# Attention scores of a two-branch decoder trunk: two 128-row products a head in place of three 64-row ones

## The chip, the cores and the metric

One Trainium2 chip, of which one core runs the kernel. The time is the device time of one execution in microseconds; the kernel before took 1076.8 us (median of three runs, 1076.33 to 1079.78).

## What is computed

One layer of a trunk: a half-weighted SwiGLU feed-forward, a token mixer, a second feed-forward, on 512 tokens of width 1024 with 16 meta tokens ahead. Only the mixer bears on the change. It projects the normalised tokens to queries, keys and values of eight "fox" heads (forgetting attention over all earlier tokens) and to eight query and two key/value heads of a sliding window of 128, all of width 64:

```
qa = rms_norm(qa.reshape(b, p, FOX_HEADS, HEAD_DIM), fox_q_norm)
ka = rms_norm(ka.reshape(b, p, FOX_HEADS, HEAD_DIM), fox_k_norm)
...
s = jnp.einsum('bqhd,bkhd->bhqk', qi, k, preferred_element_type=jnp.float32) * scale
s = s + cqi[..., :, None] - c_k[:, :, None, :]
...
s_band = jnp.einsum('bnqgrd,bnkgd->bngrqk', qb, kb, preferred_element_type=jnp.float32) * scale + bias_band[None]
...
y = jax.nn.sigmoid(ga) * (o_fox @ w_branch_fox) + jax.nn.sigmoid(gb) * (o_swa @ w_branch_swa)
```

## The kernel before

Everything is float32, and TensorE is fed with a shorter type. So each operand a is kept as two: its part aH (`hi`, line 130: ScalarE rounds it) and its rest aL = a - aH (`lo`, line 136: VectorE subtracts). A product a b is the sum of three in one PSUM bank: aH bH + aH bL + aL bH (`prod`, line 297).

The mixer's work is a list of small steps. A chunk (`tok_chunk`, line 1025) projects 256 columns for the five token tiles, two steps (half tiles) of twelve 128-row products each; the values (`v_chunk`), the keys and queries (`qk_chunk`, line 1120) and the sliding keys and values (`kv_chunk`) are chunks. The last step of a query or key chunk (`finish`) transposes the normalised heads on TensorE, so that a head's 64 features lie in rows: two heads share 128 rows, the even one in rows 0 to 63, the odd one in 64 to 127. From there the parts are rounded and the rests taken, 128 rows at a time, with the gains.

A fox unit (`fox_pair`, line 1249) takes a pair p of heads and two query blocks: the wide ones (ip = 1) see blocks 2 and 3, the narrow ones 0 and 1. There are four wide and four narrow units, p = 0 and 1 on the first chunks (f0), p = 2 and 3 on the second (f1). A sliding unit (`swa_unit`, line 1431) takes four heads and one block; there are eight. A unit's `scores` are products of 64 rows; VectorE then adds the biases and finds the minimum of the negated scores (L1310, L1460), ScalarE takes the exponent (L1209), VectorE divides (L1212), TensorE transposes the result (L1350, L1473), it is split in part and rest, and the values are multiplied (L1359 to L1365, L1488, L1490). Fox scores are written in lines 1289 to 1299 with the two heads in turn; the sliding ones go through `prod`, so they stand under L301, L302 and L304 with kH, kL and qH in their names.

`weave` (line 57) mixes the units' steps with steps of chunks that are needed later (`fills`, line 1628): TensorE has projections to do while a unit's softmax runs on the other engines. There are four such parts: the first two pairs of heads, the other two, and two groups of four sliding heads. A scheduler then sets each engine's order, and each engine goes through its own in that order. SyncE's queue loads the weights (L206, L252); a load waits there until its buffer is free, and what is behind it waits too.

Two buffers matter besides: zA (8 rows of 512 a partition, tag z), where the gates are put from the third part on and whose last two rows held masks, and oA (tag o), the attention's result.

## Time and profile before

| | us |
|---|---|
| runs | 1076.33, 1076.8, 1079.78 |
| the profiled execution | 1077.47 |
| its span, first to last instruction | 1075.7 |
| TensorE busy | 1064.0 |
| VectorE busy | 891.9 |
| ScalarE busy | 655.0 |
| granted TensorE clock (share of full speed) | 0.997 |

Times in the trace count from the span's start. PE is TensorE, PEld its weight loads, DVE VectorE, ACT ScalarE, POOL GpSimd, SP SyncE. In the order of time a row is start, length, engine, line, operation, output and input tiles, forms; a matmul's length includes its way through the array, so neighbours overlap, and the step from start to start tells what one costs. "64*128" is a product of 64 rows. In the windows stand the window, its length, and busy time with the number of instructions for PE, PEld, DVE, ACT and POOL, then the granted clock, the DMA share and GB/s. A row of waits has who waited, at what line, for whom: us in total, times, longest. A row of a group has its count, busy time, mean ns of one, and idle time before it. A DMA row has its count, size, and median time to landing.

### The profile page before, as it was taken

What the parts mean: (1) busy time and instruction counts of PE and PEld (TensorE: products, weight loads), DVE (VectorE), ACT (ScalarE), POOL (GpSimd) and SP (SyncE); (2) the same over time, 40 slices, a digit from 0 to 9 for tenths busy, and PEclk for the clock granted to TensorE, in tenths of its full rate; (3) what the DMA queues carried; (4) which work ended last, traced back from release to release, by engine and by line L of the source; (5) the groups of instructions that cost most, each with busy time, mean ns of one, the idle gap of its engine ahead of it and who ended that gap; (6) DMA issues with size and microseconds to landing.
All of it is one profiled execution on the core that took longest, in us unless ns stands there. A gap on an engine that the chain in (4) does not pass through costs nothing.

```text
span 1075.7 us, 22259 instructions
## 1 busy us (share of the span) xinstructions
PE 1064.0 (99%) x8515; PEld 1031.8 (96%) x8515; DVE 891.9 (83%) x1725; ACT 655.0 (61%) x1235; POOL 212.9 (20%) x281
## 2 busy tenths in 40 slices
PE   9999999999999999999999999999999999999998
PEld 8999999999999998999878799999999999999998
DVE  6988878988889678789897799878989788887895
ACT  7676456656666455556667866555665466745664
POOL 3011111121124442232200110001122211221120
PEclk9999999999999999999999999999999999999999
DMA  8787777688776414222311874557688777887763
GB/s 281 195 217 167 187 195 192 154 215 219 174 181 179 124 61 119 76 65 64 98 59 40 239 177 134 186 193 201 166 205 182 184 193 177 180 194 196 158 125 102
DMA packets 112570, 173.57 MB, mean 161 GB/s; under 512 B 10880, under 2 KB 59264, under 8 KB 112208
## 3 DMA queue, kind: packets, MB, share of 16 engines
q1 hardware_dynamic: 74032, 122.03, 35.5%
q0 software_dynamic: 29040, 37.83, 22.6%
q10 hardware_dynamic: 9392, 12.29, 3.7%
q8 instruction: 66, 1.08, 0.4%
q14 instruction: 40, 0.33, 0.1%
HBM read 167.89 MB, written 6.32 MB: 162 GB/s over the span
## 4 chain that ended last, share of the span: by engine, by line
PE 47%; DVE 4%; ACT 2%; DMA 1%; issue 1%; POOL 0%; ACTq 0%; DVEq 0%; POOLq 0%
PE ps L301 8%; PE ps L304 8%; PE ps L302 8%; PE pt L301 7%; PE pt L302 7%; PE pt L304 7%; DMA raw<-in_wout_dram 1%; DVE wl L140 1%; ACT wh L133 1%; ACT t L1209 1%; DVE pL L140 1%; PE ps L1473 0%; PE ps L1936 0%; DVE S L140 0%; PE pt L1473 0%
## 5 line engine op out<-in xcount | busy, mean ns | idle before, releaser
L301 PE MATMUL ps<-x,wh 128*128 128x256 f32 (+2 forms) x768 | 220.1, 287 | 0.1
L302 PE MATMUL ps<-x,wh 128*128 128x256 f32 (+2 forms) x768 | 219.4, 286 | 0.5 <-DVE x L142 0.4
L304 PE MATMUL ps<-x,wl 128*128 128x256 f32 (+2 forms) x768 | 219.4, 286 | 0.0
L140 DVE TENSOR_TENSOR wl<-raw,wh 128x1024 fp32r<-128x1024 f32 (+3 forms) x125 | 149.9, 1200 | 40.7 <-ACT wh L133 39.5
L133 ACT CAST wh<-raw 128x1024 fp32r<-128x1024 f32 (+3 forms) x125 | 128.4, 1029 | 86.1 <-PE ps L302 50.9
L301 PEld LDWEIGHTS ps<-x,wh 128*128 128x128 f32 x768 | 145.3, 189 | 1.4 <-ACT pt L529 0.3
L302 PEld LDWEIGHTS ps<-x,wh 128*128 128x128 f32 x768 | 145.1, 189 | 1.4 <-DVE x L142 0.9
L304 PEld LDWEIGHTS ps<-x,wl 128*128 128x128 f32 x768 | 145.2, 189 | 0.9
L301 PE MATMUL pt<-x,wh 128*128 128x256 f32 (+2 forms) x424 | 125.3, 297 | 0.2 <-ACT wh L133 0.2
L304 PE MATMUL pt<-x,wl 128*128 128x256 f32 (+2 forms) x424 | 124.5, 294 | 0.0
L302 PE MATMUL pt<-x,wh 128*128 128x256 f32 (+2 forms) x392 | 112.5, 287 | 0.0
L133 ACT CAST wh<-tc 128x1024 fp32r<-128x1024 f32 (+1 forms) x70 | 71.8, 1026 | 64.3 <-DVE tc L234 55.1
L140 DVE TENSOR_TENSOR wl<-tc,wh 128x1024 fp32r<-128x1024 f32 (+1 forms) x70 | 83.5, 1193 | 32.4 <-ACT wh L133 32.2
L301 PE MATMUL ps<-acts,wh 128*128 128x264 f32 (+1 forms) x352 | 100.5, 285 | 0.1
L304 PE MATMUL ps<-acts,wl 128*128 128x264 f32 (+1 forms) x352 | 99.8, 284 | 0.0
L302 PE MATMUL ps<-acts,wh 128*128 128x264 f32 (+1 forms) x352 | 99.5, 283 | 0.0
L140 DVE TENSOR_TENSOR wl<-rawC,wh 128x1024 fp32r<-128x1024 f32 (+1 forms) x70 | 84.2, 1202 | 5.9 <-ACT wh L133 5.5
L133 ACT CAST wh<-rawC 128x1024 fp32r<-128x1024 f32 (+1 forms) x70 | 71.6, 1023 | 22.8 <-PE pt L302 16.9
L301 PEld LDWEIGHTS pt<-x,wh 128*128 128x128 f32 x424 | 79.9, 189 | 2.6 <-ACT wh L133 0.4
L304 PEld LDWEIGHTS pt<-x,wl 128*128 128x128 f32 x424 | 79.8, 188 | 2.1
L302 PEld LDWEIGHTS pt<-x,wh 128*128 128x128 f32 x392 | 73.7, 188 | 0.6
L301 PEld LDWEIGHTS ps<-acts,wh 128*128 128x128 f32 x352 | 66.5, 189 | 0.7 <-DVE h2T L918 0.3
(442 smaller groups left out, 3241.8 us busy)
## 6 DMA issues: line engine op xcount, KB each, us to landing
rawC<-in_w1i_dram SPq DMA_DIRECT2D x20, 512.0 KB, 4.5
raw<-in_w1i_dram SPq DMA_DIRECT2D x40, 256.0 KB, 4.0
raw<-in_w2i_dram SPq DMA_DIRECT2D x40, 256.0 KB, 3.5
rawC<-in_w2i_dram SPq DMA_DIRECT2D x20, 512.0 KB, 4.4
raw<-in_wm_dram SPq DMA_DIRECT2D x18, 512.0 KB, 4.4
raw<-in_wout_dram SPq DMA_DIRECT2D x16, 512.0 KB, 4.4
rawD<-in_w1i_dram SPq DMA_DIRECT2D x20, 256.0 KB, 4.0
raw<-in_w1i_dram POOLq DMA_DIRECT2D x20, 256.0 KB, 5.2
```

The lines of the kernel that those rows point to most:

```text
L133: return A.copy(o, i)
L140: return V.tensor_tensor(out=o, in0=i, in1=h, op=ALU.subtract)
L301: PE.matmul(ps, sH, mH, start=first, stop=False, **more)
L302: PE.matmul(ps, sH, mL, start=False, stop=False, **more)
L304: shared["mm"] = PE.matmul(ps, sL, mH, start=False, stop=last, **more)
L1209: shared["exp"] = A.activation(t, t, AF.Exp, bias=nmx, scale=-1.0, accum_out=l[:, j : j + 1])
```

## The change

Stacked operands: the keys of each fox head get a tile of 128 rows of their own, the part in the head's own 64 rows and the rest in the other 64. The fox queries get their part in both halves (tile qH) and their rest in both halves (tile qz). The score is then qH times the stack (aH bH + aH bL at once) and qz times the stack (aL bH, and aL bL besides). For the sliding heads it is the queries that are stacked (part and rest), and the keys, which stood in both halves before, are multiplied as part (kH) and as rest (kL). So a head has two products of 128 rows: 144 in all (80 fox, 64 sliding) for 216 of 64 rows (120 and 96).

Both halves of the fox queries are made by rounding one and copying it to the other half by DMA, four copies a chunk on SyncE's queue. The stacked rest is written by VectorE from one half of the rows to the other. Roundings and rests are taken 64 rows at a time. qz lies where zA was; zA is taken when a gate first needs it, and the masks' last rows move to oA. Three value steps (`va[5:8]`) go ahead of the fox scores, and three steps of the sliding keys and values (`kv[LAG : LAG + 3]`) from the second fill to the end of the first.

```
--- before.py
+++ after.py
@@ -982,7 +982,16 @@
     banks["turn"] = False
     kp = ctx.enter_context(tc.tile_pool(name="keep", bufs=1))
     oA = kp.tile([P, 2, 4, S], F32, tag="o", name="oA")
-    zA = kp.tile([P, KD, S], F32, tag="z", name="zA")
+    qz = kp.tile([P, 2 * 4, S], F32R, tag="z", name="qz")
+
+    class Later_z:
+
+        def __getitem__(self, at):
+            if "z" not in shared:
+                shared["z"] = kp.tile([P, KD, S], F32, tag="z", name="zA")
+            return shared["z"][at]
+
+    zA = Later_z()
     stM = ExitStack()
     mp = stM.enter_context(tc.tile_pool(name="mix", bufs=2))
     r1 = cp.tile([P, NB + 1], F32, name="r1")
@@ -1117,15 +1126,21 @@
 
         return tok_chunk(alloc, range(NB + 1), lambda i, ps: v_evac(box["v"], i, ps))
 
-    def qk_chunk(box, tag, tiles, gcol):
+    def stack(o, other, src, gain, hh):
+
+        a, b = (slice(HD * x, HD * x + HD) for x in (hh, other))
+        hi(o[a], src[a], gain[a])
+        if other != hh:
+            lo(o[b], src[a], o[a], gain[a])
+
+    def qk_chunk(box, tag, tiles, gcol, rests=None):
 
         off = M if tag == "q" else 0
         qn = {}
 
         def alloc():
             if off:
-                q = new("qH", [P, 4, S])
-                box[tag] = q[:, :2], q[:, 2:]
+                box[tag] = new("qH", [P, 4, S]), rests
             else:
                 box[tag] = tuple(new(tag + x, [P, 2, 4 * P + 3 * M + 4]) for x in "HL")
 
@@ -1151,20 +1166,30 @@
                     src = qn[i][:, 2 * pr : 2 * pr + 2].rearrange("p h d -> p (h d)")
                     c = P * (i - 1 if off else NB - i)
                     PE.transpose(ps[:, c : c + P], src, ident)
-                d = (slice(None), pr, slice(M - off, M - off + S))
-                hi(dH[d], ps, g)
-                lo(dL[d], ps, dH[d], g)
+                for hh in range(2):
+                    hb = slice(HD * hh, HD * hh + HD)
+                    if rests is not None:
+                        h = 2 * pr + hh
+                        hi(dH[hb, h], ps[hb], g[hb])
+                        lo(dL[hb, h], ps[hb], dH[hb, h], g[hb])
+                    elif off:
+                        stack(dH[:, 2 * pr + hh], 1 - hh, ps, g, hh)
+                    else:
+                        stack(box[tag][hh][:, pr, M : M + S], 1 - hh, ps, g, hh)
+            if rests is not None:
+                for hh in range(2):
+                    for t in (dH, dL):
+                        t = t.bitcast(F32).rearrange("p (a b) c -> p a b c", b=2)
+                        to, frm = (slice(HD * x, HD * x + HD) for x in (1 - hh, hh))
+                        SP.dma_start(t[to, :, hh], t[frm, :, hh])
             if off:
                 return
             pm = psum()
             for pr in range(2):
                 PE.transpose(pm[:, P * pr : P * pr + P], qn[0][:, 2 * pr : 2 * pr + 2].rearrange("p h d -> p (h d)"), ident)
             for hh, c in ((0, T), (1, 0)):
-                hb = slice(HD * hh, HD * hh + HD)
-                d = (hb, slice(None), slice(c, c + M))
-                src = pm[hb, : 2 * P].rearrange("p (r c) -> p r c", c=P)[:, :, :M]
-                hi(dH[d], src, g[hb])
-                lo(dL[d], src, dH[d], g[hb])
+                src = pm[:, : 2 * P].rearrange("p (r c) -> p r c", c=P)[:, :, :M]
+                stack(box[tag][hh][:, :, c : c + M], 1 - hh, src, g, hh)
 
         return tok_chunk(alloc, tiles, evac, finish)
 
@@ -1221,7 +1246,7 @@
         return bass.AP(tensor=tile_.tensor, offset=tile_.offset + c0, ap=[list(tile_.ap[0]), [step, 2], [1, n]])
 
     def load_cb(p):
-        main, last = new("cb", [P, 1092], F32), zA[:, 6 + p % 2]
+        main, last = new("cb", [P, 1092], F32), oA[:, 1, p % 2]
         cbs[p] = main, last
         for t, n, c0, step in ((main, MAIN, P, T - P), (last, 2 * P, 0, T + LAST)):
             src = bass.AP(tensor=cbd.tensor, offset=cbd.offset + 2 * p * T + c0, ap=[[0, P], [step, 2], [1, n]])
@@ -1286,15 +1311,15 @@
                 i = 2 * ip + b
                 for pi in range(len(block[0])):
                     two = pss[b, pi] = psum(), psum()
-                    for qx, kx in ((0, 0), (0, 1), (1, 0)):
-                        for hb, ps, spans in zip(half, two, block):
-                            c0, w = spans[pi][:2]
+                    for hh, (ps, spans) in enumerate(zip(two, block)):
+                        c0, w = spans[pi][:2]
+                        for x in range(2):
                             PE.matmul(
                                 ps[:, :w],
-                                q[qx][hb, hp, P * i : P * i + P],
-                                k[kx][hb, hp, c0 : c0 + w],
-                                start=qx + kx == 0,
-                                stop=qx == 1,
+                                q[x][:, 2 * hp + hh, P * i : P * i + P],
+                                k[hh][:, hp, c0 : c0 + w],
+                                start=x == 0,
+                                stop=x == 1,
                             )
             parts = []
             for hh in range(2):
@@ -1445,11 +1470,15 @@
                 t2 = room[:, 546 * hp : 546 * hp + 546]
                 for hh in (2 * hp, 2 * hp + 1):
                     h = 4 * g + hh
-                    hb = slice(64 * (hh % 2), 64 * (hh % 2) + 64)
                     ps = psum()
-                    sq = (hb, hp, slice(P * i, P * i + P))
-                    sk = (hb, g, slice(k0, k0 + w))
-                    prod([(ps[:, :w], k[0][sk], k[1][sk])], q[0][sq], q[1][sq], True, True)
+                    for x in range(2):
+                        PE.matmul(
+                            ps[:, :w],
+                            q[0][:, hh, P * i : P * i + P],
+                            k[x][:, g, k0 : k0 + w],
+                            start=x == 0,
+                            stop=x == 1,
+                        )
                     t = t2[:, 273 * (hh % 2) : 273 * (hh % 2) + nk]
                     nmx = new("nmx", [P, 2], F32, 8)
                     init = 3.0e38
@@ -1541,9 +1570,9 @@
     log_forget()
     tc.keep_in_program_order(A.activation(warm, nhalf, AF.Exp))
     ka = qk_chunk(f0, "k", every, 1)
-    qa = qk_chunk(f0, "q", toks, 0)
+    qa = qk_chunk(f0, "q", toks, 0, qz[:, :4])
     va = v_chunk(f1)
-    run(ka[:-1] + qa[:LAG] + ka[-1:] + [forget_sums, lambda: load_cb(0)] + qa[LAG:-1] + va[:3] + [lambda: mask_late(0)] + qa[-1:] + va[3:5])
+    run(ka[:-1] + qa[:LAG] + ka[-1:] + [forget_sums, lambda: load_cb(0)] + qa[LAG:-1] + va[:3] + [lambda: mask_late(0)] + qa[-1:] + va[3:8])
     spread(r1, [(i, P * (i - 1), P) for i in toks], rb1)
 
     def pre(p, ip):
@@ -1622,12 +1651,12 @@
         [swa_unit(sw, q2, 0, i, swa_pre.get(i, nothing)) for i in range(NB)],
         [swa_unit(sw, q3, 1, i, nothing) for i in range(NB)],
     ]
-    k1, q1 = qk_chunk(f1, "k", every, 1), qk_chunk(f1, "q", toks, 0)
+    k1, q1 = qk_chunk(f1, "k", every, 1), qk_chunk(f1, "q", toks, 0, qz[:, 4:])
     kv, qb0, qb1 = kv_chunk(sw), qk_chunk(q2, "q", toks, 2), qk_chunk(q3, "q", toks, 2)
 
     fills = [
-        va[5:] + k1[:-1] + q1[:LAG] + k1[-1:] + q1[LAG:-1] + kv[:LAG] + q1[-1:],
-        kv[LAG:-1] + qb0[:LAG] + kv[-1:] + qb0[LAG:-1] + qb1[:2] + qb0[-1:] + qb1[2:4],
+        va[8:] + k1[:-1] + q1[:LAG] + k1[-1:] + q1[LAG:-1] + kv[:LAG] + q1[-1:] + kv[LAG : LAG + 3],
+        kv[LAG + 3 : -1] + qb0[:LAG] + kv[-1:] + qb0[LAG:-1] + qb1[:2] + qb0[-1:] + qb1[2:4],
         qb1[4:-1] + gates[:LAG] + qb1[-1:] + gates[LAG:],
         foxes,
     ]
```

The narrow unit of the second pair of heads on TensorE (kH, kL, qH the fox keys and queries; ps and pt PSUM banks; wh, wl and x a projection's weights and tokens). Before:

```order
L1292 MATMUL ps_6171<-kH_5068,qH_5245 128x256
L1292 MATMUL ps_6179<-kH_5068,qH_5245 128x272
L1292 MATMUL ps_6179<-kL_5069,qH_5245 128x272
L1292 MATMUL ps_6179<-kH_5068,qH_5245 128x272
L301 MATMUL pt_6096<-wh_5759,x_4306 128x256
L302 MATMUL pt_6096<-wl_5760,x_4306 128x256
L304 MATMUL pt_6096<-wh_5759,x_4310 128x256
L301 MATMUL pt_6096<-wh_5759,x_4306 128x256
L1292 MATMUL pt_6172<-kH_5068,qH_5245 128x256
L1292 MATMUL pt_6172<-kL_5069,qH_5245 128x256
L1292 MATMUL pt_6172<-kH_5068,qH_5245 128x256
L302 MATMUL pt_6096<-wl_5760,x_4306 128x256
```

and in the changed kernel, where kH is the even head's stack and kL the odd one's:

```order
L304 MATMUL pt_6152<-wh_5700,x_4311 128x256
L1317 MATMUL pt_6224<-kH_5068,qH_5245 128x256
L1317 MATMUL pt_6224<-kH_5068,qz 128x256
L1317 MATMUL ps_6225<-kL_5069,qH_5245 128x256
L1317 MATMUL ps_6225<-kL_5069,qz 128x256
L1317 MATMUL pt_6230<-kH_5068,qH_5245 128x272
L1317 MATMUL pt_6230<-kH_5068,qz 128x272
L1317 MATMUL ps_6231<-kL_5069,qH_5245 128x272
L1317 MATMUL ps_6231<-kL_5069,qz 128x272
L301 MATMUL pt_6256<-wh_5694,x_4304 128x256
```

The two heads' products, which stood in pieces between projection products, stand in one row, each head's two together.

The wide unit of the third pair, the first to use the second query chunk, on TensorE. Before:

```order
L304 MATMUL pt_6403<-wh_6049,x_4310 128x256
L301 MATMUL pt_6403<-wh_6049,x_4307 128x256
L1292 MATMUL ps_6438<-kH_5751,qH_6042 128x400
L1292 MATMUL pt_6439<-kH_5751,qH_6042 128x400
L1292 MATMUL ps_6438<-kL_5752,qH_6042 128x400
L1292 MATMUL pt_6439<-kL_5752,qH_6042 128x400
L1292 MATMUL ps_6446<-kH_5751,qH_6042 128x272
```

and now (pH, pL and v belong to the unit before):

```order
L304 MATMUL ps_6458<-wh_6028,x_4311 128x256
L1317 MATMUL pt_6501<-kH_5692,qH_6021 128x400
L1317 MATMUL pt_6507<-kH_5692,qH_6021 128x272
L1317 MATMUL pt_6513<-kH_5692,qH_6021 128x256
L1384 MATMUL pt_6541<-pH_6445,v_4889 128x256
L1389 MATMUL pt_6541<-pH_6451,v_4889 128x256
L1390 MATMUL pt_6541<-pL_6452,v_4889 128x256
L1389 MATMUL pt_6541<-pH_6451,v_4889 128x128
L1317 MATMUL pt_6501<-kH_5692,qz 128x400
```

The products with qH stand first, those with qz after some of the unit before. Between the chunk's last transpose and the first of these scores stand 36 projection products and 5 transposes; before, there were six projection products.

SyncE's queue around the first query chunk. Before:

```order
L252 DMA raw_5441<-in_wm_dram 128x1024
L252 DMA raw_5447<-in_wm_dram 128x1024
L252 DMA raw_5757<-in_wm_dram 128x1024
L252 DMA raw_5763<-in_wm_dram 128x1024
L252 DMA raw_6047<-in_wm_dram 128x1024
```

and now:

```order
L252 DMA raw_5445<-in_wm_dram 128x1024
L252 DMA raw_5451<-in_wm_dram 128x1024
L1184 DMA qH_5245<-qH_5245 64x2x512
L1184 DMA qz<-qz 64x2x512
L1184 DMA qH_5245<-qH_5245 64x2x512
L1184 DMA qz<-qz 64x2x512
L252 DMA raw_5698<-in_wm_dram 128x1024
```

Four copies stand between two pairs of weight loads.

## The prediction, made before the changed kernel was run

> **What bounds the kernel now.** I read the page first, then the table of windows over the mixer's attention stages, TensorE's waits there, and the order of time of TensorE around the score products, which the change rewrites. A line of the page:
>
> ```profile
> PE 1064.0 (99%) x8515; PEld 1031.8 (96%) x8515; DVE 891.9 (83%) x1725; ACT 655.0 (61%) x1235; POOL 212.9 (20%) x281
> ```
>
> TensorE is busy nearly always. The windows are: the time from the first fox scores to those of the third head pair, from there to the first sliding scores, and on to the second group of sliding heads; the last window is a part of the third, in which VectorE is fullest.
>
> ```profile
> 413.20:471.60 58.40, 57.33 (x475) 53.88 (x474) 46.26 (x136) 32.07 (x80) 16.48 (x39) 1.00 0.27 83
> 471.60:520.40 48.80, 47.58 (x404) 44.98 (x403) 43.82 (x137) 30.54 (x81) 14.18 (x27) 1.00 0.24 67
> 520.40:560.80 40.40, 39.97 (x253) 32.86 (x252) 35.51 (x104) 26.95 (x66) 3.02 (x3) 1.00 0.17 53
> 545.00:560.00 15.00, 15.00 (x83) 11.93 (x82) 13.94 (x35) 8.89 (x22) 0.00 (x0) 1.00 0.23 71
> ```
>
> After the length stand the busy times of TensorE, its weight loads, VectorE, ScalarE and GpSimd. TensorE sets the pace in all of them, but VectorE is at 0.79, 0.90 and 0.88 of the first three, and at 0.93 of the last. TensorE's waits from 413 to 600 us are small:
>
> ```profile
> PE pt L1365 <- DVE pL L140: 1.0, 3, 0.5
> PE ps L1292 <- DVE qn L1073: 0.5, 1, 0.5
> ```
>
> So a microsecond of TensorE saved is a microsecond of the kernel, until VectorE is late.
>
> **The products.** Before, a fox unit has 18 (wide, ip = 1) or 12 (narrow) products of 64 rows, a sliding unit 12. The heads' products stand in turn. A narrow unit in order of time:
>
> ```profile
> 483.34 0.28 PE L304 MATMUL ps<-wh,x 128*128 128x256 f32 x1
> 483.55 0.38 PE L1292 MATMUL ps<-kH,qH 64*128 64x256 f32 x1
> 483.55 0.38 PE L1292 MATMUL pt<-kH,qH 64*128 64x256 f32 x1
> 483.77 0.28 PE L1292 MATMUL ps<-kL,qH 64*128 64x256 f32 x1
> ...
> 484.26 0.28 PE L1292 MATMUL ps<-kH,qH 64*128 64x272 f32 x1
> 484.26 0.28 PE L1292 MATMUL pt<-kH,qH 64*128 64x272 f32 x1
> 484.48 0.39 PE L301 MATMUL ps<-wh,x 128*128 128x256 f32 x1
> 484.70 0.28 PE L302 MATMUL ps<-wl,x 128*128 128x256 f32 x1
> 484.82 0.28 PE L304 MATMUL ps<-wh,x 128*128 128x256 f32 x1
> ```
>
> The two heads start at the same time: a pair costs one step. Steps (start to start) are 0.12 us between products of one kind (484.70 to 484.82; 0.118 in my count for 256 columns, 0.125 for 272), and 0.21 to 0.22 at four places: into the group, at its first step, out of it, and after that. So 6 steps of pairs cost 0.73 us and the change of kind 0.40. The new unit has 8 steps of one kind with all around them: from 483.34 to 484.70 it takes 1.36 now, and 2 x 0.118 + 4 x 0.118 + 4 x 0.125 = 1.21 then: 0.15 less. That is my estimate from steps of 128-row products; no new product is in this trace. A sliding unit likewise:
>
> ```profile
> 532.45 0.40 PE L304 MATMUL ps<-x,wl 128*128 128x512 f32 x1
> 532.78 0.39 PE L301 MATMUL pt<-kH,qH 64*128 64x274 f32 x1
> ...
> 533.74 0.51 PE L301 MATMUL ps<-x,wh 128*128 128x512 f32 x1
> 534.08 0.40 PE L302 MATMUL ps<-x,wh 128*128 128x512 f32 x1
> 534.31 0.39 PE L304 MATMUL ps<-x,wl 128*128 128x512 f32 x1
> ```
>
> 1.63 now, 2 x 0.232 + 8 x 0.126 = 1.47 then: 0.16 less. Three narrow fox units and eight sliding ones of this tidy kind give 11 x 0.155 = 1.7.
>
> The Trainium skill ("TensorE: Matmul & The Clock Gate", the table for one's kernel) speaks against the change: products with few rows should lie in distinct row groups, where they run side by side. The starts at 483.55 agree. "TensorEngine Tiling (Array Packing)", key properties, adds that a change of tiling mode drains the engine; the 0.40 agrees with that. By the first rule alone the sum would be the third rival's.
>
> Where the scheduler took a unit apart, pairs are lost and the change of kind is paid again. The narrow unit of the second pair stood so on TensorE, in four pieces among projection products (the section on the change shows the two orders; there a head's two products now stand together), and being taken apart costs the new products nothing. What it cost before:
>
> ```profile
> 452.26 0.38 PE L1292 MATMUL ps<-kH,qH 64*128 64x256 f32 x1
> ...
> 454.20 0.28 PE L301 MATMUL pt<-wh,x 128*128 128x256 f32 x1
> 454.41 0.39 PE L1292 MATMUL pt<-kH,qH 64*128 64x256 f32 x1
> ...
> 454.96 0.39 PE L302 MATMUL pt<-wl,x 128*128 128x256 f32 x1
> 455.18 0.28 PE L304 MATMUL pt<-wh,x 128*128 128x256 f32 x1
> ...
> 457.13 0.39 PE L302 MATMUL ps<-wl,x 128*128 128x256 f32 x1
> ```
>
> From 454.20 to 455.18 three products took 0.98 less two ordinary steps, 0.74; four such pieces (2, 4, 3 and 3 products, 452.26 to 457.13) make 2.96, against 0.97 for eight new steps: 2.0 less. Of the four wide units the first is tidy and gains nothing (12 steps for 9 pairs and 0.40). The third:
>
> ```profile
> 471.35 0.28 PE L301 MATMUL pt<-wh,x 128*128 128x256 f32 x1
> 471.88 0.34 PE L1292 MATMUL pt<-kL,qH 64*128 64x400 f32 x1
> 472.06 0.76 PE L1292 MATMUL ps<-kH,qH 64*128 64x272 f32 x2
> 473.81 0.28 PE L304 MATMUL pt<-wh,x 128*128 128x256 f32 x1
> ```
>
> 2.46 less two steps is 2.22; 4 steps of 0.18 (400 columns, 471.88 to 472.06), 4 of 0.125 and 4 of 0.118 are 1.69: 0.53 less. I take the same for the other two that came apart: 1.6. Sum for TensorE: -1.7 - 2.0 - 1.6 = **-5.3 us**.
>
> **What is added.** Each half of the rows gets its own rounding and its own rest, so each of six chunks (four fox, two sliding) has four of each for two:
>
> ```profile
> L134 ACT ACTIVATE qH<-ps,gq 128x512 fp32r<-128x512 f32 x4 | 2.8, 689 | 1.8 <-PE ps L1153 1.8
> L142 DVE SCALAR_TENSOR_TENSOR qH<-ps,gq,qH 128x512 fp32r<-128x512 f32 x4 | 3.0, 745 | 1.3 <-ACT qH L134 1.3
> ```
>
> A piece of 64 rows has the same 512 columns; I take the same length, less an overlap of some 0.07 between neighbours: 12 more of each, 8 us on VectorE and 7 us on ScalarE. ScalarE is at 0.55 to 0.67, and hides it. VectorE is the question. Three half-tile steps of the values (36 products, 36 x 0.118 = 4.2 us of TensorE) now run ahead of the fox scores, and three of the sliding keys move from the second stage into the first. The first stage so has as many products as before; it gains VectorE's work of two chunks (2.6) and two token tiles, which at 46.26 of 58.40 it can take. The second stage loses 4.2 us and, of the 5.3, two wide units' 0.53 and two narrow ones' 0.155: TensorE could be through in 48.8 - 4.2 - 1.4 = 43.2. VectorE's 43.82 there gain 1.3 for one chunk and lose about 0.7 with the keys' tokens (my count of the rows moved): 44.4. VectorE becomes the longer of the two. How dense can it go? It had 0.90 there and 0.93 from 545 to 560, with TensorE never idle; the end on the other side is 1.00. I take 0.965, the middle of the densest stretch seen and that end: 46.0, so **+2.8 us** against 43.2; bounds are +1.2 (1.00) and +6.1 (0.90).
>
> **The copies.** SyncE's queue gets four copies of 256 KB after each fox query chunk. They stand between loads of weights for later chunks. No weight is near due behind them. TensorE's scores wait for their landing. On TensorE the second query chunk's last transposes stand 36 projection products and 5 transposes ahead of the first score, 4.8 us. Before, a score followed the chunk at once and needed no DMA; now the parts' scores come first and the rests' (qz) later. Transfers of this size landed in
>
> ```profile
> zA<-cbd ACTq DMA_DIRECT2D x4, 256.0 KB, 5.5
> cb<-biasd ACTq DMA_DIRECT2D x2, 256.0 KB, 2.8
> ```
>
> Two roundings (some 1.5 us with their start) and 2.8 or 5.5 are 4.3 or 7.0: nothing, or 2.2 late. I take +0.1: the first chunk has 57 products in between and is covered at either end, and of the second only what is over 3.3 us of landing shows. Without that cover they would cost their full 4.3.
>
> The queries' rests in z and the masks in o cost nothing: the gates that next use z come after the last scores.
>
> Sum: -5.3 + 2.8 + 0.1 = **-2.4 us**. The profiled execution took 1077.47 (span 1075.7), 0.7 over the median; from the median, 1076.8 - 2.4 = **1074.4**. About 0.3%, 3.2 us, is what a measurement can tell from no change, so this lies within it.
>
> **Rivals.** *VectorE keeps up* (0.38): it runs at 0.99 or more, or leans into the next stage. For it: 0.93 without a TensorE wait, and the small waits above. The loss is 0 to 1.6: 1071.5 to 1073.1.
>
> *VectorE's gaps stay* (0.11): its idle time is the chain of a unit (scores, minimum, exponent, scaling, transposes), not slack. Then the second stage takes 44.4 / 0.90 = 49.3 (+6.1), the third (35.51 + 1.3) / 0.88 = 41.8 against 40.4 - 0.6 = 39.8 (+2.0): -5.3 + 8.1 = +2.8, and with late copies +5.0: 1079.6 to 1081.8. In the second stage alone it cancels the gain when the share stays below 44.4 / 48.5 = 0.915. Against it: twelve projection products stand between most dependent steps, and the waits were few.
>
> *The steps stay wide* (0.04): the 0.40 belongs to new weights and banks, not to the kind, and only the pairs count. Then 216 products in 108 pairs become 144 single steps, 36 x 0.122 = +4.4: 1081.2. Against it: steps among 128-row products with new weights each time are 0.12.
>
> **How the numbers follow.** My own case has 0.47 and reaches from -3.2 to +1. Faster by over 0.3%: the first rival, 0.38. Slower: 0.12, the third rival and most of the second. Within: 0.50. The range 1071.3 to 1078.6 takes in the first rival's end and leaves out some 0.15.
>
> **What would show it.** Right: in the changed profile score products start 0.12 to 0.18 us apart, with no 0.21 around them; 144 of them; VectorE at 0.95 or more between the third pair's scores and the sliding ones, a stage of about 46 us, with TensorE waiting for VectorE in it. Wrong: that stage at 43 to 44 us (first rival) or 49 (second); waits for DMA of more than 1 us ahead of scores; steps of 0.2 between score products (third).

## The result, and the profile after

The changed kernel took 1087.27 us (median of six runs, 1086.59 to 1089.17), the kernel before 1076.53 beside it: ratio 1.0099, with an interval of 1.0088 to 1.011. So it is about 10.7 us slower, where 1074.4 was forecast and the range ended at 1078.6. The profiled execution took 1088.3, its span is 1086.4.

The page of the changed kernel, its line of busy times. TensorE has 72 products fewer and is busy 1.2 us longer:

```profile
PE 1065.2 (98%) x8443; PEld 1037.1 (95%) x8443; DVE 900.7 (83%) x1737; ACT 662.9 (61%) x1247; POOL 214.9 (20%) x281
```

The table of windows over the changed kernel: up to the first fox scores, to the third pair's, to the sliding ones, to the second sliding group; then the 8 us in which the first copies are under way, and two stretches of its own:

```profile
384.00:419.48 35.48, 32.62 (x271) 31.51 (x270) 25.30 (x60) 17.20 (x31) 14.42 (x24) 1.00 0.43 117
419.48:479.44 59.96, 56.44 (x445) 54.80 (x446) 47.50 (x140) 34.37 (x83) 16.13 (x36) 0.94 0.31 90
479.44:528.23 48.79, 45.98 (x357) 43.71 (x355) 41.72 (x131) 30.67 (x80) 14.34 (x27) 0.97 0.28 79
528.23:570.14 41.91, 40.52 (x244) 34.63 (x242) 38.35 (x108) 29.17 (x71) 3.02 (x3) 1.00 0.15 51
412.00:420.00 8.00, 5.82 (x47) 5.39 (x45) 3.12 (x6) 1.49 (x3) 2.65 (x7) 0.95 1.05 270
419.31:426.14 6.83, 5.27 (x19) 4.51 (x20) 1.59 (x7) 1.55 (x4) 0.68 (x2) 0.50 0.29 62
494.41:497.82 3.41, 3.41 (x18) 3.41 (x17) 3.41 (x16) 1.92 (x8) 1.80 (x2) 0.51 0.03 7
```

The first scores start at 419.48 and not at 413.20: 6.3 us later, of which the 36 moved products explain 4.2. The first stage then takes 59.96 for 58.40 (with 7 projection products fewer, 296 for 303), the second 48.79 for 48.80 (with 29 fewer, 192 for 221). The fourth row of the table, the third stage, ends 0.6 us into the second sliding group, whose first product starts at 569.54; up to there the stage takes 41.3, for 40.4. And there is something that the mixer before has nowhere: two stretches in which the granted clock is 0.5, 6.83 and 3.41 us long. The profile before does have one of 3.4 us, but at 12.2 us, in the first feed-forward; four kernels below that move no steps (e2, e13, e14, e15) do not have it and begin the fox scores 0.7 to 1.2 us earlier.

TensorE's longest waits between 384 and 700 us:

```profile
PE ps L1317 <- DMA qH<-qH: 2.2, 1, 2.2
PE pt L301 <- DVE kL L142: 1.5, 1, 1.5
PE pt L302 <- issue: 1.5, 1, 1.5
PE ps L1502 <- DVE t L1237: 1.1, 2, 0.7
PE ps L1362 <- DVE qn L1082: 0.9, 1, 0.9
...
PE ps L1317 <- DMA qz<-qz: 0.7, 1, 0.7
PE pt L1317 <- DMA qH<-qH: 0.7, 1, 0.7
```

Three of them are waits for the copies at the first scores. In the order of time on TensorE there:

```profile
419.48 0.67 PE L1317 MATMUL ps<-kH,qH 128*128 128x400 f32 x1 [2.18 <-DMA qH<-qH]
420.86 0.67 PE L1317 MATMUL ps<-kH,qz 128*128 128x400 f32 x1 [0.71 <-DMA qz<-qz]
421.33 0.43 PE L1317 MATMUL ps<-kH,qH 128*128 128x272 f32 x1
422.44 0.68 PE L1317 MATMUL pt<-kL,qH 128*128 128x400 f32 x1 [0.69 <-DMA qH<-qH]
...
424.01 0.41 PE L301 MATMUL ps<-wh,x 128*128 128x256 f32 x1
424.22 0.41 PE L302 MATMUL ps<-wl,x 128*128 128x256 f32 x1
...
426.80 0.28 PE L301 MATMUL ps<-wh,x 128*128 128x256 f32 x1
426.92 0.28 PE L302 MATMUL ps<-wl,x 128*128 128x256 f32 x1
```

A step of 256 columns is 0.21 us at 424 and 0.12 at 426.8: half clock, then full. The waits are 3.58 together. What the half clock adds, an estimate made step by step against the same shapes at full clock, is 2.0 in the first stretch and 1.5 in the second. The issues of DMAs between 404 and 428 us, with the median time to landing, tell why the copies were late:

```profile
raw<-in_wm_dram SPq DMA_DIRECT2D x2, 512.0 KB, 6.6
cb<-cbd ACTq DMA_DIRECT2D x2, 400.0 KB, 6.9
...
qH<-qH SPq DMA_DIRECT2D x2, 256.0 KB, 9.1
qz<-qz SPq DMA_DIRECT2D x2, 256.0 KB, 9.4
```

They share the DMA engines with a load of weights and with the masks that ScalarE's queue fetches, at a DMA share of 1.05 (the window from 412 to 420 above). The Trainium skill ("DMA: Bandwidth & Descriptors", queues, rings and completion order) says that SyncE's and ScalarE's queues are rings on the same 16 engines, which take turns by packets; that agrees.

The products themselves do what was foreseen. A wide unit of the second pair, in order of time:

```profile
445.92 0.28 PE L304 MATMUL ps<-wh,x 128*128 128x256 f32 x1
446.03 0.35 PE L1317 MATMUL pt<-kH,qH 128*128 128x400 f32 x1
446.21 0.34 PE L1317 MATMUL pt<-kH,qz 128*128 128x400 f32 x1
...
447.50 0.28 PE L1317 MATMUL ps<-kL,qH 128*128 128x256 f32 x1
447.61 0.28 PE L1317 MATMUL ps<-kL,qz 128*128 128x256 f32 x1
447.73 0.28 PE L301 MATMUL ps<-wh,x 128*128 128x256 f32 x1
```

Twelve products in 1.70 us, 0.18 and 0.12 apart, with no wider step into the group or out of it.

### The profile page after: what moved, and what is told of

The parts are those of the page before. It is cut to its first block, busy times and chain, and to the rows that moved or that the text cites. A ratio compares the mean times of both kernels' runs of the same rounds, so it can differ in the third digit from the quotient of the medians.

```text
span 1086.4 us, 22156 instructions
## 1 busy us (share of the span) xinstructions
PE 1065.2 (98%) x8443; PEld 1037.1 (95%) x8443; DVE 900.7 (83%) x1737; ACT 662.9 (61%) x1247; POOL 214.9 (20%) x281
## 4 chain that ended last, share of the span: by engine, by line
PE 45%; DVE 3%; ACT 2%; DMA 2%; issue 1%; ACTq 0%; DVEq 0%
PE ps L301 7%; PE ps L304 7%; PE ps L302 7%; PE pt L301 6%; PE pt L302 6%; PE pt L304 6%; DMA raw<-in_wout_dram 1%; ACT wh L133 1%; DMA xg<-h1d 1%; DVE wl L140 1%; ACT xg L1757 0%; PE ps L1502 0%; ACT t L1234 0%; PE ps L1965 0%; DMA h2T<-h1d 0%
## 5 line engine op out<-in xcount | busy, mean ns | idle before, releaser
L301 PE MATMUL ps<-x,wh 128*128 128x256 f32 (+2 forms) x768 | 219.6, 286 | 0.1
L301 PEld LDWEIGHTS ps<-x,wh 128*128 128x128 f32 x768 | 144.9, 189 | 1.4 <-ACT hT L686 0.3
L301 PE MATMUL pt<-x,wh 128*128 128x256 f32 (+2 forms) x424 | 125.5, 296 | 0.2 <-DVE qH L142 0.2
L301 PE MATMUL ps<-acts,wh 128*128 128x264 f32 (+1 forms) x352 | 100.5, 286 | 0.1
L301 PEld LDWEIGHTS pt<-x,wh 128*128 128x128 f32 x424 | 80.0, 189 | 2.4 <-DVE qH L142 0.4
L301 PEld LDWEIGHTS ps<-acts,wh 128*128 128x128 f32 x352 | 66.6, 189 | 0.7 <-DVE h2T L918 0.3
```

The lines of the kernel that those rows point to most:

```text
L301: PE.matmul(ps, sH, mH, start=first, stop=False, **more)
```

## The experiments

Three theories stood at the start. A: the loss is the copies, by their wait and by the half clock behind it. B: it is the roundings and rests taken by halves, which keep VectorE and the PSUM banks longer. C: it is the moved steps. Later runs took up the products, the sliding heads and the ways of filling the other half. All times are medians in us; before is the kernel before on the same chip.

| run | time | before | ratio and interval |
|---|---|---|---|
| e1 no copies | 1081.75 | 1076.57 | 1.0053 (1.0032 to 1.0073) |
| e2 before, halved roundings | 1081.64 | 1076.57 | 1.0055 (1.0038 to 1.0071) |
| e3 before, moved steps | 1077.69 | 1076.57 | 1.0011 (1.0001 to 1.002) |
| e4 sliding stack only | 1080.4 | 1076.57 | 1.0036 (1.0023 to 1.0049) |
| e5 more cover | 1085.5 | 1077.26 | 1.0067 (1.0041 to 1.0092) |
| e6 dummy work | 1079.06 | 1077.26 | 1.0014 (1.0004 to 1.0023) |
| e7 halved, sliding queries | 1078.97 | 1077.26 | 1.0011 (1.0001 to 1.002) |
| e8 fox stack, more cover | 1082.39 | 1077.26 | 1.0041 (1.0029 to 1.0053) |
| e9 GpSimd copies | 1085.51 | 1076.61 | 1.0081 (1.006 to 1.0103) |
| e10 fox stack, GpSimd, unmoved | 1079.85 | 1076.61 | 1.0029 (1.0019 to 1.0039) |
| e11 halved from an SBUF copy | 1083.04 | 1076.61 | 1.0058 (1.0043 to 1.0073) |
| e12 GpSimd copies, full width | 1078.11 | 1076.61 | 1.0018 (1.0008 to 1.0029) |
| e13 products only | 1072.75 | 1076.67 | 0.9965 (0.9952 to 0.9978) |
| e14 fox products only | 1071.05 | 1076.67 | 0.9954 (0.9938 to 0.997) |
| e15 products and halved | 1075.83 | 1076.67 | 0.9996 (0.9987 to 1.0005) |
| e16 fox stack, copies by head | 1080.98 | 1077.68 | 1.003 (1.0019 to 1.004) |
| e17 the same, moved steps | 1078.03 | 1077.68 | 1.0006 (0.9997 to 1.0015) |
| e18 fox stack, written twice | 1080.58 | 1076.68 | 1.003 (1.0018 to 1.0042) |

**e1: the changed kernel without the copies;** GpSimd clears the other halves when the tile is taken.

```
+                        G.memset(t[HD * (1 - hh) : HD * (2 - hh), :, hh], 0.0)
...
-                        SP.dma_start(t[to, :, hh], t[frm, :, hh])
```

> The changed kernel without the eight copies between the halves of the rows; the half that they would fill is set to zero by GpSimd before the chunk's projections, so the scores lack the products of the queries' parts with the keys' rests. Products, roundings and fills are as in the changed kernel. Theory A (the copies land late: 3.6 us of waits ahead of the first fox unit, and the half clock of 6.8 us that follows them): 6 to 7 us faster than the changed kernel, 1080 to 1081, the first unit's products 0.12 to 0.18 us apart. Theory B (the roundings by halves keep VectorE and the PSUM banks longer, so that TensorE waits all through the attention): only the 3.6 us of waits go, 1083 to 1084. Theory C (the moved fill steps leave the second stage too little to do beside the softmax): 1080 to 1084 as well, but the stage from the third pair's first score to the sliding scores stays at 48 to 49 us.

1081.75, 5.5 under the changed kernel: nearer to A's 1080 to 1081 than to B's 1083 to 1084, though the interval reaches both; the stage that C wanted at 48 to 49 took 46.90. No stretch at half clock is left in the mixer. One row of its waits is the price of the clearing, early in the mixer (GpSimd clears, VectorE waits 2.65 us for its result at 379.94 where it waits 1.32 in the changed kernel, and is then late with a weight's rest); the others are still there without copies:

```profile
PE pt L301 <- DVE kL L142: 1.5, 1, 1.5
PE pt L302 <- issue: 1.4, 1, 1.4
PE ps L302 <- DVE wl L140: 1.4, 1, 1.4
```

With that 1.4 taken off, the copies cost 6.9 (6.4 by the ratios), close to the 3.58 + 3.5 = 7.1 of the trace. But 3.8 over before remain.

**e2: the kernel before with roundings and rests by halves.**

```
-                d = (slice(None), pr, slice(M - off, M - off + S))
-                hi(dH[d], ps, g)
-                lo(dL[d], ps, dH[d], g)
+                for hh in range(2):
+                    hb = slice(HD * hh, HD * hh + HD)
+                    d = (hb, pr, slice(M - off, M - off + S))
+                    hi(dH[d], ps[hb], g[hb])
+                    lo(dL[d], ps[hb], dH[d], g[hb])
```

> The kernel before, with the parts and rests of fox keys and of all queries taken 64 rows at a time (twelve more roundings and rests); nothing else. Theory B: 3 to 4 us slower than before, 1080. Theories A and C: within 1 us of before, 1076 to 1077.5.

1081.64, 5.1 over: B holds beside A. Neither alone explains the result.

**e3: the kernel before with the moved steps alone** (`va[3:8]` and `kv[LAG : LAG + 3]` as in the change).

> The kernel before, with the three value steps ahead of the fox scores and the three sliding key steps at the end of the first fill, as the change has them; nothing else. Theory C: 3 to 5 us slower than before, 1080 to 1081.5, with the stage from the third pair's first score to the sliding scores at 47 to 49 us in spite of 36 products fewer. Theories A and B: within 1 us of before, that stage at 44.5 to 45.5 us.

1.1 over, where C gave 3 to 5: as the main cause C falls. Its stage did take 47.56 us, as C said, but the one ahead of it got 1.9 shorter (56.48). What the moved steps do beside the rest is another matter (below).

**e4: the kernel before with the sliding heads stacked, nothing else** (four roundings and four rests of 64 rows a query chunk, two products a head).

> The kernel before, with the sliding heads' scores alone by two 128-row products (queries stacked, two chunks rounded by halves); fox scores, fills and buffers as before. Theories A and C: the sliding units' 1.3 us are gained, 1075 to 1076. Theory B: two chunks' roundings cost about a third of 3 to 4 us, so no change, 1076.5 to 1077.5.

3.8 over, more than any theory gave. **e7** takes only the halved roundings of it:

```
+                for hb in (slice(0, HD), slice(HD, P)) if gcol == 2 else (slice(None),):
```

> The kernel before, with roundings and rests taken 64 rows at a time for the sliding queries alone (4 more of each). All twelve cost 5.1 us. If each costs alike, a third of it: 1078.0 to 1078.7. If the cost lies where the trace of that kernel jumped (1.7 us at the second sliding query chunk, 540 us, and 1.0 behind the attention): 1079 to 1080. Its difference to the kernel with sliding queries stacked (3.8 us over before) is what the products themselves bring there: by the prediction's 0.16 a unit that one would be 1.3 us faster.

1.7 over, about a third of e2's 5.1. So about 2 of the 3.8 came with the sliding products, which were to save 1.3. e13 and e14 show where.

**e5: more work between the copies and the scores.**

```
-... qa[LAG:-1] + va[:3] + [lambda: mask_late(0)] + qa[-1:] + va[3:8])
+... qa[LAG:-1] + va[:2] + qa[-1:] + va[2:3] + [lambda: mask_late(0)] + va[3:])
```

> The changed kernel with more work between the copies and the first scores: all value steps stand ahead of the scores (two more, 24 products, 2.8 us), and the step that issues the first copies stands one value step earlier. Nothing is left out or added. Theory A (the first copies land too late, TensorE stands still, and its clock is then halved for some microseconds): no wait for the copies at the first scores, no stretch at half clock, and 1080.5 to 1083. Rival (what the kernel without copies gained came from less traffic on the DMA engines, not from the wait): 1085.5 to 1088.

1085.5: the expected number was missed, though the waits tell that it was the cover and not the theory that was too small. Its waits:

```profile
PE ps L1317 <- DMA qz<-qz: 1.5, 1, 1.5
...
PE ps L1317 <- DMA qH<-qH: 1.4, 1, 1.4
```

The copies were issued at the same time (411.0; 24 products more ran behind them), and landed in 8.2 and 9.6 us. The rival's time came out, but its reason does not hold against e9, which has no copies by DMA and is no faster than this one. The clock was halved in both places again: 0.91 from 412 to 430 and from 490 to 510.

**e6: as many more roundings and rests as the change adds, for nobody.**

```
+                A.activation(zA[up, 4], dH[once_more].bitcast(F32), AF.Identity, scale=g[up])
+                V.scalar_tensor_tensor(out=zA[up, 5], in0=dL[once_more].bitcast(F32), scalar=g[up], in1=dH[once_more].bitcast(F32), op0=ALU.mult, op1=ALU.subtract)
```

> The kernel before, with one more rounding on ScalarE and one more rest on VectorE, of 64 rows by 512 from SBUF into unused memory, behind each of the twelve pairs of them (12 more of each, the number that the change adds). Nobody waits for their results and no PSUM bank is held for them. Theory W (the halved roundings cost by their work on VectorE and ScalarE, which are in turn late for TensorE): about what the halved roundings cost, 1080 to 1083. Theory H (they cost because the bank stays held, and the query or key is ready later, by the second half): 1076 to 1078.

1.8 over, against 5.1 for e2, and the intervals lie apart: as many steps on the same engines (reading SBUF and not the bank), but at a third of the price when no one waits for them. **e11** asks what the waiting is for, the bank or the result:

```
+                copied = zA[:, 4 + pr]
+                A.copy(copied, ps)
+                ps = copied
```

> The kernel before with halved roundings and rests (5.1 over before), whose source is not the PSUM bank: ScalarE first copies the bank to SBUF (12 copies of 128 by 512 more), so that the bank is held by one copy and no longer by four steps, while parts and rests are ready later than ever. Theory HB (the held bank costs): 1077 to 1079. Theory HL (the lateness of parts and rests costs): 1081.5 to 1085.

1083.04: with the bank free after one copy nothing is won. That speaks for HL, that parts and rests are ready later in e2; but ScalarE's 12 added copies may have their part in the time, which this run does not separate, so HL is not shown.

**e8: fox stack and more cover, the sliding heads as before.**

> The changed kernel with two things set right: the cover for the first copies as in the kernel with all value steps ahead, and the sliding heads as before (no stack there). If the costs found so far add up (1087.3, less 5.5 for the copies, less 3.8 for the sliding stack), 1077 to 1079.5, so about the kernel before and no gain: the fox products' saving is used up by their own halved roundings. If the products' saving comes through once VectorE has room, below 1075.

1082.39, above both numbers: the costs found so far do not add up. The sliding heads give back 3.1 against e5, as e4 let expect; the copies are still late (waits of 0.41 and 1.60 for them).

**e9: the copies on GpSimd.**

```
-                        SP.dma_start(t[to, :, hh], t[frm, :, hh])
+                        G.tensor_copy(t[to, :, hh], t[frm, :, hh].bitcast(F32))
```

> The changed kernel with the fox queries' copies to the other half made by GpSimd (four copies of 64 by 1024 in SBUF a chunk) and not by DMA. Theory A (the copies' whole price is that they land late among the other loads): no wait for a DMA at the first fox scores, no stretch at half clock, and 7 us less than the changed kernel, 1079.5 to 1081.5, a little under the kernel without copies (1081.75), whose fillings of the halves cost 1.3. Rival (any way of filling the other half is too late, since the scores follow the roundings closely): a wait for GpSimd in its place and 1083 to 1087.

1085.51: the rival's number. Each copy takes 1.03 us of GpSimd, four stand in a row, and TensorE waits for them and has 0.91 of its clock from 412 to 430:

```profile
PE ps L1317 <- POOL qz L1184: 0.9, 2, 0.5
...
PE pt L1317 <- POOL qH L1184: 0.7, 1, 0.7
...
PE pt L1317 <- POOL qz L1184: 0.5, 1, 0.5
```

**e12: the same with full-width roundings and rests.**

> As the kernel with GpSimd copies, but with roundings and rests 128 rows at a time as before: both halves of the rows go to the same place, so the parts and rests of the odd heads stand in the wrong half and the scores are not the reference's; products, copies and their number are those of the changed kernel. Theory H (the halved steps cost about 4 in the changed kernel too): 4 to 5.5 less than the kernel with GpSimd copies, 1075 to 1077, which is then what stacked products alone are worth, 0 to 1.5 us under the kernel before. If the products' saving of 5.3 comes through once the rest is gone: 1071 to 1073.

1078.11, which is 6.8 under e9 by the ratios, more than theory H's 4 to 5.5. But the clock differs too: from 412 to 430 us e9 has 0.91 and e12 1.00, some 1.6 of the 6.8 by estimate (0.09 of 18 us), so that about 5.2 are left for the halved steps, no more than in e2. And e12 stays over the kernel before, not under it.

**e13, e14, e15: the products by themselves.** Only the score products are exchanged (e14: the fox ones), and the meta columns of the keys are split over all 128 rows, which these products read; e15 adds e2's halved steps.

```
-                    for qx, kx in ((0, 0), (0, 1), (1, 0)):
-                        for hb, ps, spans in zip(half, two, block):
...
+                    for hh, (ps, spans) in enumerate(zip(two, block)):
+                        c0, w = spans[pi][:2]
+                        for x in range(2):
                             PE.matmul(
                                 ps[:, :w],
...
+                                q[x][:, hp, P * i : P * i + P],
+                                k[hh][:, hp, c0 : c0 + w],
+                                start=x == 0,
+                                stop=x == 1,
```

> The kernel before with nothing changed but the score products: two of 128 rows a head (144) on the parts and rests as they lie there, for three of 64 rows. Roundings, order of the steps, buffers are as before, there are no copies; the scores are not the reference's, since the other head's rows are multiplied in. By the prediction's count, -5.3: 1071.3. By the steps counted in the changed kernel's trace, -3.3, and the stall at the first product of the split attention result (1.4, seen wherever the sliding heads have such products): 1074.7. Rival (VectorE's chain sets the time of the attention stages, TensorE's saving only becomes waiting): 1076 to 1077.5.

> The same for the fox heads alone (80 products of 128 rows for 120 of 64), the sliding ones as before; scores of the fox heads not the reference's. By the prediction's count -4.0 (three narrow tidy units 0.5, one in pieces 2.0, wide ones 1.6): 1072.6. If the stages wait for VectorE instead: 1075.5 to 1077. No stall at the split attention result.

> The products of 128 rows alone, and roundings and rests 64 rows at a time (12 more of each), with no copies and no moved steps; scores not the reference's, as there. If the halved steps cost what they cost beside the old products, 5.1 over the products alone. If more beside faster products (6.8 between the two kernels with GpSimd copies), because TensorE then comes earlier to where it waits for VectorE: 6 to 8 over.

With nothing added the products save 3.8 by the ratio, the fox ones alone 5.0. VectorE's chain does not take it back. The two differ behind the attention. The first minimum search of the last sliding unit starts at 585.75 us before, at 578.84 in e13 (6.9 earlier) and at 579.32 in e14 (6.4 earlier); the spans are 1075.7, 1072.9 (2.8 shorter) and 1069.2 (6.5 shorter). The order of time of TensorE in e13, where the split attention result is first multiplied, and some 20 us later:

```profile
595.84 0.39 PE L301 MATMUL pt<-x,wh 128*128 128x512 f32 x1
597.64 0.47 PE L302 MATMUL pt<-oLs,wh 128*128 128x512 f32 x1 [1.42 <-issue]
...
619.26 0.39 PE L301 MATMUL ps<-S,wh 128*128 128x256 f32 x1 [2.09 <-ACT pt L529]
...
619.85 0.41 PE L302 MATMUL ps<-S,wh 128*128 128x256 f32 x1
620.06 0.42 PE L304 MATMUL ps<-S,wl 128*128 128x256 f32 x1
620.27 0.41 PE L301 MATMUL ps<-S,wh 128*128 128x256 f32 x1
```

The window behind it stands at 0.92 of the clock in e13 (the first row), and at 1.00 in e14:

```profile
620.00:640.00 20.00, 20.00 (x159) 20.00 (x158) 17.65 (x31) 12.38 (x25) 3.46 (x4) 0.92 0.72 174
```

```profile
620.00:640.00 20.00, 20.00 (x171) 20.00 (x170) 19.43 (x38) 13.33 (x27) 3.46 (x4) 1.00 0.77 197
```

The profile writes "issue" for the wait of 1.42, but VectorE's rest for it (oLs, the first of four from 596.75) had just ended. In all eight kernels with sliding heads in 128-row products (the changed one, e1, e4, e5, e9, e12, e13, e15) TensorE's order has 30 products between the attention's last value product and this one, and each has this stall of 1.42 to 1.47; in the other twelve it has 35, and none has it. That the scheduler spends five fill products earlier because the sliding units look shorter to it is a reading of this; no run shows its reason. The wait of 2.09 and the half clock are not as regular: e15 has the wait too (2.25) and keeps its clock, and of e13's five executions the two with a mean clock of 1.0 took 1071.36 and 1071.95, the others 1072.75 to 1074.66. e15 is 3.3 over e13, less than either number that was expected.

**e10, e16, e17, e18: fox stack alone, the other half filled otherwise.** e10 has e9's copies and no moved steps; e16 copies each head behind its own rounding; e17 adds the moved steps; e18 has no copies, ScalarE and VectorE write both halves from the bank:

```
+                        for to in (hb, slice(HD * (1 - hh), HD * (1 - hh) + HD)):
+                            hi(dH[to, h], ps[hb], g[hb])
+                            lo(dL[to, h], ps[hb], dH[hb, h], g[hb])
```

> Fox stack alone with copies by GpSimd: the sliding heads as before, and no steps moved between the parts. If the costs add up (the kernel with GpSimd copies, less 3 for the sliding stack, less 1 for the moved steps), 1076 to 1077.5, no different from the kernel before. If the moved steps were needed to hide the copies, 1078 to 1080 with waits at the first scores.

> Fox stack alone, no moved steps, copies by GpSimd as before, but head by head right behind the head's own rounding and rest (eight of 64 by 512 a chunk for four of twice that), so that the first pair of heads needs to wait for four copies and not for all. If the two waits for GpSimd (3.33 and 1.33) go: 1079.85 less 4.7, 1075.2, between 1074 and 1076.2, under the kernel before. If the copies are still late: 1077.5 to 1080, with waits for GpSimd ahead of the fox scores.

> The same with the change's moved steps (three value steps ahead of the scores, three sliding key steps to the end of the first part). If the copies are already in time without them, the moved steps only add their own 0 to 1.1: 1075 to 1077. If they are late without them: 1075 to 1076.5 here and 1077.5 or more there.

> Fox stack alone, no moved steps, and no copies: ScalarE and VectorE write the fox queries' part and rest into both halves straight from the bank (16 more steps of 64 rows on each engine than before in all four fox chunks, 8 of them in the place of the copies). If steps cost what the halved ones cost beside the new products (3.2 for 12, so 0.27 each) and the fox products save 5.6: 1076.6 - 5.6 + 4.3 = 1075.3, between 1074 and 1077. If VectorE is the bound at the first scores: 1078 or more, with waits of TensorE for it there.

e10 and e16 miss the adding up: TensorE waits for GpSimd ahead of the first scores (3.33 in e10; the row is e16's), and its clock is 0.91 from 412 to 430 us:

```profile
PE pt L1317 <- POOL qH L1182: 2.8, 1, 2.8
```

e16 and e17 come out over the ranges that were expected, on a chip on which the kernel before took 1077.68. Still, by the ratio e17 is the best of the kernels that compute the reference with stacked operands, and no different from the kernel before. e18 is too late as well, by work: waits for ScalarE's and VectorE's results, and 0.83 of the clock from 470 to 490. No version beat the kernel before while computing what it must.

## Why the prediction was wrong

**The products (-5.3).** Right in kind and near in size for the fox heads: e14 shows -5.0 (-6.7 to -3.2) for -4.0. For the sliding heads it failed: e4 less e7, and e13 less e14, are losses of 1 to 2.7 where -1.3 stood, though the intervals of e13 and e14 overlap. The units themselves got a little shorter (from the first sliding unit's minimum search to the last's 64.66 us before, 64.61 in e14, 64.23 in e13), but the scheduler's order behind the attention changed with them. The prediction compared the orders only in the stages that the change touches.

**The copies (+0.1) are the step that failed most.** "The first chunk has 57 products in between and is covered at either end" took landing times of 2.8 and 5.5 from rows of other moments. Here the DMA share was 1.05 in the 8 us that the copies were under way, and they took 8.4 to 9.7. By e1 they cost 5.5 and, without the price of the clearing, 6.9. Half of that is no wait at all but the clock behind the waits, which the prediction had nowhere. "No weight is near due behind them" was true; what shared the engines with them mattered. The second chunk's copies, with less beside them, landed in 3.3 to 3.8 us, and no wait for them stands in the trace.

**Halved steps and VectorE (+2.8).** Size nearly right (e15 less e13: 3.3), reason wrong. The stage was to be 46 us with VectorE at 0.95 or more; it took 48.79 with VectorE at 41.72 / 48.79 = 0.86, and 46.90 with 0.89 in e1, where no half clock falls into it. VectorE was not full; single results came late. That is what e6 against e2 says too. The second rival's stage lengths (49.3 and 41.8) came near (48.79 and 41.3), but for the second stage that is luck, as the half clock is in it and e1 has 46.90; and e13 and e14 speak against its ground, idle time of VectorE that cannot shrink: with nothing added the time saved on TensorE does arrive.

**The moved steps ("which at 46.26 of 58.40 it can take").** Alone 1.1 (e3). They also took 29 products out of the second stage and 7 out of the first, not 36 and none. Beside halved steps they seem dearer. The windows of e15 (halved, not moved) and of e1 (halved and moved), 430 to 520 us:

```profile
430.00:470.00 40.00, 38.67 (x320) 37.80 (x320) 33.88 (x96) 24.07 (x56) 14.32 (x28) 1.00 0.27 87
470.00:490.00 20.00, 19.67 (x159) 18.89 (x160) 18.34 (x64) 12.59 (x36) 5.93 (x14) 1.00 0.19 52
490.00:520.00 30.00, 30.00 (x251) 29.48 (x250) 27.64 (x93) 20.14 (x54) 8.67 (x14) 1.00 0.25 75
```

```profile
430.00:470.00 40.00, 37.99 (x320) 37.47 (x320) 33.10 (x98) 23.38 (x59) 12.83 (x28) 1.00 0.27 84
470.00:490.00 20.00, 18.04 (x143) 16.94 (x142) 17.99 (x55) 12.61 (x31) 5.79 (x13) 1.00 0.10 37
490.00:520.00 30.00, 29.31 (x242) 28.40 (x241) 26.74 (x84) 19.99 (x53) 10.11 (x16) 1.00 0.31 90
```

TensorE idles 1.66 there in e15 and 4.66 in e1 (counted from the first fox scores to the sliding ones, 1.8 and 4.8). The wait of 1.5 for a key's rest (L301 for kL) stands in the kernels that have both (the changed one, e1, e9, e17) and not in e15, e16 or e18, which move nothing, nor in e3 and e12, whose steps are not halved; e5 and e8, which move more, have one of 1.3 for a query's norm in its place.

**The account.** Before to e13: -3.8. To e15: +3.3. To e1 without its clearing: 6.1 - 1.4 = +4.7, of which 1.2 is the moved steps' own price; the other 3.5 may come of moved and halved steps together. e9 less e12, without e9's half clock 5.2 for the halved steps beside moved ones where 3.3 stands without them, has the same sign but gives 1.9. To the changed kernel: 1.0099 - 1.0053 = 5.0, and 1.4: +6.4. That the parts add up to 10.6 of 10.7 proves nothing, since each step starts where the one before ends; what carries weight is each difference, and each is uncertain by 1.5 to 2.5. So the copies are shown as the largest part and the halved steps as the second; the joint price of moved and halved steps is argued.

**What stays open.** e12 is 2.3 over what products, moved steps and its waits for GpSimd (2.2) make. Why the second stretch at half clock, at 494 us, comes: it is there in e5 and e8 and gone in e1 and e9, which have much the same small waits ahead of it. How large the joint price of moved and halved steps is: e15 with the moved steps and nothing else was not run. And whether a full bank or a late result costs more was tried with a copy that itself adds work.

## What to carry to other kernels

Fewer products of full rows can save what their steps say, and for the fox heads did, as long as the operands cost nothing; the price lay in making the operands. Cost a copy by a landing time from a row of the same moment, with the DMA share that stands there, and reckon that a TensorE wait of 2 us can cost as much again by the clock behind it. When an edit changes the length of a stage, compare each engine's order to the end of the program, since a scheduler may move fill work far behind the edit.

## What was not expected of the hardware

Half clock followed short idle times, and not always. Of five waits of TensorE of 2 us or more, four had it behind them, for 3.4 us or twice that: 2.18 (the changed kernel, 6.83 us at 0.50), 2.83 (e16), 3.33 (e10), and 2.09 (e13, whose 256-column steps are 0.21 from 619.85 on). The fifth, 2.25 at the same product in e15, did not: the steps behind it are 0.12. Single waits of 1.42 to 1.58 did not (e1, e4, e13, e17), but two of 1.35 and 1.48 within 2 us did (e5), two of 1.13 and 0.58 (e18), and three of 0.53 to 0.65 (e9), where two of 0.94 and 0.54 did not (e12). The kernel before has 3.4 us of it from 12.2 us on, with no wait over 0.36 ahead. So the length of one wait does not decide it. The Trainium skill ("TensorE: Matmul & The Clock Gate", Part 1) gives a free-running window of 3413 ns, with which the lengths 3.41 and 6.83 agree, and half clock after at least one idle window; here less idle time was enough, and the measurement decides.

A wait put down to "issue" ended 0.2 us after VectorE had finished the rest that the product reads: the trace's release can be missing where the order and the other engine's end tell it.
